# Attention scores in the two halves of the array's rows: three passes of 64 rows in place of two passes of 128

## The chip, the cores and the metric

The kernel runs on one core of a Trainium2 chip. The metric is the device time of one execution in microseconds (us). Before the change the median of three runs is 1358.63 us, the lowest 1357.41 and the highest 1358.8.

## What is computed

Two transformer blocks over 512 tokens of width 1024. The first has a stick-breaking attention with 16 heads of 64, a cross attention over 256 memory rows and a convolutional feed-forward; the second has three branches (a recurrent one with 8 heads of 64, a short convolution, a pooling) that are gated, merged and projected. The change touches the stick-breaking attention alone:

```
def stick_breaking_core(q, k, v):              # 16 heads of 64
    for start in range(0, seq, 128):
        end = start + 128
        z = einsum('bhtd,bhsd->bhts', q[start:end], k[:end]) * 64 ** -0.5
        earlier = arange(end)[None, :] < arange(start, end)[:, None]
        log_keep = where(earlier, log_sigmoid(-z), 0.0)
        csum = cumsum(log_keep, axis=-1)
        log_w = log_sigmoid(z) + (csum[..., -1:] - csum)
        w = where(earlier, exp(log_w), 0.0)
        outs.append(einsum('bhts,bhsd->bhtd', w, v[:end]))
```

## The kernel before

Every large product is done in three passes: an operand x is kept as two tiles of the type fp32r, its rounded value (hi) and the rest (lo), and hi·hi, hi·lo and lo·hi are added up in PSUM. `split_from` (L231) makes such a pair from PSUM: a copy on ACT for hi, a subtraction on DVE for lo. `mm3` (L217) issues the passes of a GEMM; its matmuls stand under L214. Weights arrive from memory in units of 512 KB and are split by `w_conv` (ACT L144, DVE L145), also fp32r.

**The order of the work.** The program writes its order out itself. A GEMM counts the array time that it has issued, and after each 1650 ns of it (eight matmuls of 512 columns, or 16 of 256) calls `tick` (L177). A tick advances the generators that run beside the GEMMs: each `yield n` lets n ticks pass. The numbers stand in the table `WAIT`. `drain` (L192) runs the generators to their end without GEMMs between.

**The attention.** The loop over eight pairs of heads, hp, computes q and k of a pair with two chunks of GEMM (`gemm_q`, `gemm_k`; `chunk` L245) and, over two pairs, v in four more (`gemm_v`). Then it drains the attention of the pair before and starts `attention(hp)` (L480) beside the GEMMs of the next pair. The last pair isn't drained at the start: its steps stand beside the chunks that compute the memory's keys (`ps_chunk<-memT`).

In `attention` a score is done in **two** passes of 128 rows. A head has only 64 rows, so the other 64 carry a second product: `gemm_q` puts a head's q hi into its own rows and its q lo into the other half; `gemm_k` puts k hi into both halves, and k lo into the own half beside rows that were zeroed once (`k_lo`, L435 to L437). The first pass gives hi·hi + lo·hi, the second hi·lo. For this q costs two copies on ACT of 64x512 and two subtractions on DVE, k four copies and two subtractions.

The steps of one pair, called here by these names; i is the block of 128 tokens whose scores are computed, and its product has (i+1)·128 columns:

- S1: block 1 of both heads, one bank of PSUM each
- S2 and S3 of head 0, then S2 and S3 of head 1: S2 is blocks 0 and 2 in one bank, S3 is block 3 in one bank, each at a place (a tick) of its own
- T: the transposes of the weights w, 20 of 128x128 in five groups of four, at three places; after each group a split of 128x512 on ACT and DVE
- V: the values, eight matmuls for each head, `values(0)` and `values(1)` at two places

After each S come, for each bank, a sigmoid on ACT (`keep`, L496), a scan on DVE (`r`, L498) and a subtraction on POOL (`w`, L500). Banks of PSUM: three with the tag g for GEMMs, two a, two b, one c. The scores use a, the transposes b and a, the values c and a.

Later in the kernel, in `rwkv_pair` (L1111), there are products of plain FP32 tiles that take 64 rows each, two heads by turns in the upper and the lower half of the rows, into two banks (`ps_ac`).

Of the kernel before, what the change touches and what calls it, by code (L numbers as in the profile page):

```python
# [68 lines left out]
def model_kernel(ctx: ExitStack, tc: tile.TileContext, a: dict, out: bass.AP, dbg: dict):  # L69
# [361 lines left out]

    def qk_tile(name):
        return att("qk", 7, name, dt=F32R)

    k_lo = [at.tile([P, S], F32R, name=f"kl{e}") for e in range(2)]  # L435
    for e in range(2):
        A.mul(k_lo[e][hrow(1 - e)], masks[hrow(1 - e), 0], 0.0)  # L437

    def gemm_q(ps=None):

        if ps is None:
            ps = chunk(xT)
        q = [qk_tile("q") for _ in range(2)]
        for e in range(2):
            A.copy(q[e][hrow(e)], ps[hrow(e)])
        for e in range(2):
            own = hrow(e)
            V.tensor_tensor(q[e][hrow(1 - e)], ps[own], f32(q[e][own]), ALU.subtract)
        return q

    def gemm_k(ps=None):

        if ps is None:
            ps = chunk(xT)
        k = [Split(qk_tile("kh"), lo) for lo in k_lo]
        for o in range(2):
            for e in range(2):
                A.copy(k[e].hi[hrow((e + o) % 2)], ps[hrow(e)])
        for e in range(2):
            own = hrow(e)  # L460
            V.tensor_tensor(k[e].lo[own], ps[own], f32(k[e].hi[own]), ALU.subtract)
        return k

# [16 lines left out]
    def attention(hp, q, k, vs):  # L480
        w, wT = {}, {}

        def scores(e, *parts):

            for z, part in enumerate((k[e].hi, k[e].lo)):
                for ps, i, o in parts:
                    n = (i + 1) * P
                    T.matmul(ps[:, o:o + n], q[e][:, tok(i)], part[:, 0:n],  # L488
                             start=z == 0 and o == 0, stop=z == 1 and i == parts[-1][1])

# [22 lines left out]

        pss = [bank("a", "ps_s") for _ in range(2)]
        for e in range(2):
            scores(e, (pss[e], 1, 0))
        t = weights_of(pss, 2)
        w[0, 1], w[1, 1] = (t, 0), (t, 256)
        yield wait["at0"]
        for e in range(2):  # L520
# [10 lines left out]
        def values(e):  # L531
            ps = bank("ca"[e], "ps_o")
            steps = []
            for j in range(4):
                s, n = wT[e, j]
                wid = (4 - j) * P
                lhs = vs[j][:, hp % 2, 2 * e:2 * e + 2, :].rearrange("p a d -> p (a d)")
                steps += [(z, j, lhs, part[:, n * P:n * P + wid]) for z, part in enumerate((s.hi, s.lo))]
            steps.insert(3, steps.pop(7))
            steps.insert(6, steps.pop(7))  # L540
            for z, j, lhs, part in steps:
                T.matmul(ps[:, j * P:S], lhs, part, start=(j == 0 and z == 0), stop=j == 2 and z == 1)  # L542
            own, oth = hrow(e), hrow(1 - e)
            A.copy(tmp[own], ps[oth])
            V.tensor_tensor(y[own], ps[own], tmp[own], ALU.add)
# [12 lines left out]
        values(1)  # L558
        split_to(y, yT.hi[:, hp], yT.lo[:, hp])
# [7 lines left out]
    for hp in range(NPAIR):  # L567
# [1010 lines left out]
```

## Time and profile before

| | before |
|---|---|
| median of three runs | 1358.63 us |
| the profiled execution | 1359.82 us |
| its span, first to last instruction | 1358.1 us |
| PE busy | 1328.8 us, 98% |
| weight loads (PEld) busy | 1112.2 us, 82% |
| DVE busy | 827.8 us, 61% |
| ACT busy | 527.9 us, 39% |
| POOL busy | 257.4 us, 19% |
| granted TensorE clock, mean | 0.993 |

The profile's times are in microseconds from the first instruction. PE are the matmuls and PEld the weight loads that run beside them. Matmuls overlap, so that a matmul's own length (0.39 us for 512 columns) is more than its share of the time: two that follow each other start 0.23 us apart. What a step costs is therefore read from one start to another.

### The profile page before, as it was taken

Reading aid. Unit: us, or ns where it says so; the run is one execution under the profiler, and the core shown is the slowest. Engines: PE = TensorE matmul, PEld = TensorE weight load, DVE = VectorE, ACT = ScalarE, POOL = GpSimd, SP = SyncE. Lnnn points to the kernel's source line nnn. Section 1 sums busy time; section 2 is a strip of 40 time slices with the busy share of each in tenths; the row PEclk is TensorE's granted clock in tenths of the full one; section 3 lists DMA queues with packets and bytes.
Section 4 is the critical chain, followed back from the end, with each engine's and each line's share of the span. In section 5 each row is a group of like instructions: output and inputs, shape, how many; then the busy total and the mean of one; then the engine's idle time right before and its main releaser. Section 6 shows DMA issues by size and latency. Waiting matters only on the chain.

```text
span 1358.1 us, 19442 instructions
## 1 busy us (share of the span) xinstructions
PE 1328.8 (98%) x7804; PEld 1112.2 (82%) x7804; DVE 827.8 (61%) x1425; ACT 527.9 (39%) x780; POOL 257.4 (19%) x244
## 2 busy tenths in 40 slices
PE   8999999999999999999999999999999989999997
PEld 7988888788879888888888888888878768887876
DVE  5787887765577555522556866666335567743575
ACT  6565665144423444321344235532323434222330
POOL 1333432000000434400132211200001342000230
PEclk9999999999999999999999999999999899999999
DMA  5121343242223333233234113234221223422331
GB/s 190 63 90 55 105 148 125 85 148 94 82 74 125 111 94 106 93 103 98 94 124 161 50 57 106 77 107 109 78 79 62 70 76 92 114 89 78 117 132 63
DMA packets 54666, 133.25 MB, mean 98 GB/s; under 512 B 19632, under 2 KB 21552, under 8 KB 54576
## 3 DMA queue, kind: packets, MB, share of 16 engines
q1 hardware_dynamic: 54576, 132.01, 30.7%
q8 instruction: 61, 1.00, 0.3%
q14 instruction: 29, 0.24, 0.1%
HBM read 126.48 MB, written 5.24 MB: 97 GB/s over the span
## 4 chain that ended last, share of the span: by engine, by line
PE 83%; DVE 10%; ACT 3%; DMA 2%; issue 1%; POOL 0%; DVEq 0%; SPq 0%; ACTq 0%; POOLq 0%
PE ps_chunk L214 48%; PE ps_rows L214 9%; PE ps_d L214 6%; PE ps_br L214 3%; PE ps_v L214 3%; PE ps_lead L214 3%; DVE wl L145 2%; PE ps_s L488 1%; PE ps_o L542 1%; ACT wh L144 1%; DVE lnt L650 1%; PE ps_t L510 1%; PE ps_z L214 1%; PE ps_o L214 1%; DMA wr<-in_w_xq_dram 1%
## 5 line engine op out<-in xcount | busy, mean ns | idle before, releaser
L145 DVE TENSOR_TENSOR wl<-wr,wh 128x1024 fp32r<-128x1024 f32 x196 | 251.8, 1286 | 144.5 <-ACT wh L144 143.9
L144 ACT CAST wh<-wr 128x1024 fp32r<-128x1024 f32 x196 | 204.9, 1046 | 116.9 <-PE ps_d L214 51.2
L214 PE MATMUL ps_chunk<-h3Th,wh 128*128 128x512 f32 x480 | 126.0, 398 | 0.0
L214 PE MATMUL ps_chunk<-h3Tl,wh 128*128 128x512 f32 x480 | 125.8, 397 | 0.0
L214 PE MATMUL ps_chunk<-h3Th,wl 128*128 128x512 f32 x480 | 124.3, 395 | 0.0
L872 DVE SCALAR_TENSOR_TENSOR c<-ps_chunk,colp,c 128x511 f32<-128x511 f32 x80 | 59.9, 749 | 92.2 <-ACT c L870 90.7
L878 POOL TENSOR_TENSOR c<-c 128x512 f32<-128x512 f32 x21 | 42.5, 2023 | 357.9 <-ACT c L877 209.3
L214 PEld LDWEIGHTS ps_chunk<-h3Th,wh 128*128 128x128 f32 x480 | 90.0, 190 | 21.1 <-issue 2.3
L214 PEld LDWEIGHTS ps_chunk<-h3Tl,wh 128*128 128x128 f32 x480 | 90.0, 190 | 19.8 <-issue 0.8
L214 PEld LDWEIGHTS ps_chunk<-h3Th,wl 128*128 128x128 f32 x480 | 89.6, 189 | 18.9
L214 PE MATMUL ps_chunk<-h2Th,wh 128*128 128x512 f32 x320 | 79.0, 389 | 0.0
L214 PE MATMUL ps_chunk<-h2Tl,wh 128*128 128x512 f32 x320 | 79.0, 389 | 0.0
L214 PE MATMUL ps_chunk<-h2Th,wl 128*128 128x512 f32 x320 | 79.0, 389 | 0.0
L500 POOL TENSOR_TENSOR w<-r 128x511 f32<-128x511 f32 x40 | 58.7, 1468 | 85.4 <-DVE r L498 76.7
L870 ACT ACTIVATE c<-ps_chunk,colp 128x512 f32<-128x512 f32 x40 | 31.1, 779 | 109.7 <-PE ps_chunk L214 109.7
L214 PEld LDWEIGHTS ps_chunk<-h2Th,wl 128*128 128x128 f32 x320 | 60.1, 188 | 12.5
L214 PEld LDWEIGHTS ps_chunk<-h2Tl,wh 128*128 128x128 f32 x320 | 60.1, 188 | 12.5
L214 PEld LDWEIGHTS ps_chunk<-h2Th,wh 128*128 128x128 f32 x320 | 60.0, 188 | 12.4
L498 DVE TENSOR_TENSOR_SCAN r<-keep,masks 128x512 f32<-128x512 f32 x40 | 59.8, 1509 | 12.5 <-ACT keep L496 8.0
L214 PE MATMUL ps_chunk<-xTh,wh 128*128 128x512 f32 x128 | 35.6, 402 | 5.3 <-ACT xTh L376 5.3
L214 PE MATMUL ps_d<-wh,gvb 128*128 128x512 f32 x128 | 39.7, 389 | 0.0
L496 ACT ACTIVATE keep<-ps_s 128x512 f32<-128x512 f32 (+1 forms) x48 | 24.5, 526 | 37.8 <-PE ps_s L488 37.7
(396 smaller groups left out, 2623.6 us busy)
## 6 DMA issues: line engine op xcount, KB each, us to landing
wr<-in_w_in_dram SPq DMA_DIRECT2D x65, 512.0 KB, 3.6
wr<-in_w_ff_dram SPq DMA_DIRECT2D x44, 512.0 KB, 3.6
wr<-in_w_dn_dram SPq DMA_DIRECT2D x22, 512.0 KB, 3.5
wr<-in_w_qk_dram SPq DMA_DIRECT2D x14, 512.0 KB, 3.5
wr<-in_w_br_dram SPq DMA_DIRECT2D x12, 512.0 KB, 3.5
wr<-in_w_v_dram SPq DMA_DIRECT2D x8, 512.0 KB, 3.7
wr<-in_w_xk_dram SPq DMA_DIRECT2D x8, 512.0 KB, 4.0
wr<-in_w_o_dram SPq DMA_DIRECT2D x8, 512.0 KB, 3.5
```

Of the source, the lines that this page charges most:

```text
L144: A.copy(w.hi, raw)
L145: lo_of.tensor_tensor(w.lo, raw, f32(w.hi), ALU.subtract)
L214: T.matmul(ps, l, r, start=start, stop=stop)
L488: T.matmul(ps[:, o:o + n], q[e][:, tok(i)], part[:, 0:n], start=z == 0 and o == 0, stop=z == 1 and i == parts[-1][1])
L496: A.activation(keep[:, j * n:(j + 1) * n], ps[:, 0:n], AF.Sigmoid, scale=-0.125)
L498: V.tensor_tensor_scan(r[:, ::-1], keep[:, ::-1], masks[:, m, ::-1], 1.0, ALU.mult, ALU.max)
L500: G.tensor_tensor(t[:, 0:S - 1], r[:, 1:S], r[:, 0:S - 1], ALU.subtract)
L510: T.transpose(ps[:, n], src[:, o + j * P:o + (j + 1) * P], ident)
L542: T.matmul(ps[:, j * P:S], lhs, part, start=(j == 0 and z == 0), stop=j == 2 and z == 1)
L870: A.activation(c, ps, AF.Identity, scale=cw(2), bias=col("ffb", j))
L872: V.scalar_tensor_tensor(c[:, 2 - r:S], ps[:, 0:S - 2 + r], cw(r), c[:, 2 - r:S], ALU.mult, ALU.add)
L878: (V if end else G).tensor_tensor(cv, cg, cv, ALU.mult)
```

## The change

The scores are done in three passes of 64 rows, hi·hi, hi·lo and lo·hi. Both heads of a pair are issued by turns, the even head with rows 0 to 63 and the odd one with rows 64 to 127, each into its own bank with the tag a. `gemm_q` and `gemm_k` become one `gemm_qk`, which splits the whole 128x512 with one copy and one subtraction; the zeroed tiles go. S2 and S3 are now one place each for both heads, T has two places instead of three, V has one place instead of two, and the second head's values go to a bank with the tag g. Of the table, `at2` goes from 1 to 3 and `at4` from 1 to 2. Nothing else of the program is changed.

```
-    "ss": 2, "us": 3, "ye": 4, "yo": 3, "yt": 1, "at0": 1, "at1": 1, "at2": 1, "at3": 1, "at4": 1,
+    "ss": 2, "us": 3, "ye": 4, "yo": 3, "yt": 1, "at0": 1, "at1": 1, "at2": 3, "at3": 1, "at4": 2,
...
-    k_lo = [at.tile([P, S], F32R, name=f"kl{e}") for e in range(2)]
-    for e in range(2):
-        A.mul(k_lo[e][hrow(1 - e)], masks[hrow(1 - e), 0], 0.0)
...
-        q = [qk_tile("q") for _ in range(2)]
-        for e in range(2):
-            A.copy(q[e][hrow(e)], ps[hrow(e)])
-        for e in range(2):
-            own = hrow(e)
-            V.tensor_tensor(q[e][hrow(1 - e)], ps[own], f32(q[e][own]), ALU.subtract)
-        return q
...
-        k = [Split(qk_tile("kh"), lo) for lo in k_lo]
-        for o in range(2):
-            for e in range(2):
-                A.copy(k[e].hi[hrow((e + o) % 2)], ps[hrow(e)])
-        for e in range(2):
-            own = hrow(e)
-            V.tensor_tensor(k[e].lo[own], ps[own], f32(k[e].hi[own]), ALU.subtract)
-        return k
+        s = Split(att("qk", 8, "qkh", dt=F32R), att("qk", 8, "qkl", dt=F32R))
+        split_from(ps, s.hi, s.lo)
+        return s
...
-        def scores(e, *parts):
-
-            for z, part in enumerate((k[e].hi, k[e].lo)):
-                for ps, i, o in parts:
-                    n = (i + 1) * P
-                    T.matmul(ps[:, o:o + n], q[e][:, tok(i)], part[:, 0:n],
-                             start=z == 0 and o == 0, stop=z == 1 and i == parts[-1][1])
+        def scores(*parts):
+
+
+            pss = [bank("a", "ps_s") for _ in range(2)]
+            for z, (l, r) in enumerate(((q.hi, k.hi), (q.hi, k.lo), (q.lo, k.hi))):
+                for i, o in parts:
+                    n = (i + 1) * P
+                    for e in range(2):
+                        T.matmul(pss[e][:, o:o + n], l[hrow(e), tok(i)], r[hrow(e), 0:n],
+                                 start=z == 0 and o == 0, stop=z == 2 and i == parts[-1][0])
+            return pss
...
-        for e in range(2):
-            ps = bank("a", "ps_s")
-            scores(e, (ps, 0, 0), (ps, 2, P))
+        for e, ps in enumerate(scores((0, 0), (2, P))):
             t = weights_of([ps], 0)
             w[e, 0], w[e, 2] = (t, 0), (t, P)
-            yield wait["at0"]
-            ps = bank("a", "ps_s")
-            scores(e, (ps, 3, 0))
+        yield wait["at1"]
+        for e, ps in enumerate(scores((3, 0))):
             w[e, 3] = (weights_of([ps], 1), 0)
-            yield wait["at1"] if e == 0 else wait["at2"]
...
+        yield wait["at2"]
         group("b", [(0, i, 0) for i in range(4)])
         group("b", [(0, 1, 1), (0, 2, 1), (0, 3, 1), (0, 3, 3)])
         yield wait["at3"]
         group("a", [(0, 2, 2), (0, 3, 2), (1, 2, 2), (1, 3, 2)])
-        yield wait["at3"]
+        group("a", [(1, 1, 1), (1, 2, 1), (1, 3, 1), (1, 3, 3)])
         group("b", [(1, i, 0) for i in range(4)])
-        group("a", [(1, 1, 1), (1, 2, 1), (1, 3, 1), (1, 3, 3)])
+        yield wait["at4"]
         y, tmp = att("y", 1, "y"), att("keep", 2, "yt")
-        yield wait["at4"]
-        values(0)
-        yield wait["at5"]
-        values(1)
+        order = [(z, j) for j in range(4) for z in range(2)]
+        order.insert(3, order.pop(7))
+        order.insert(6, order.pop(7))
+        for e in range(2):
+            ps = bank("cg"[e], "ps_o")
```

**On the tensor engine, at the first S1** (a piece of the difference; q and kh, kl are the tiles of before, qkh and qkl hi and lo of q and k now):

```order
 L214 MATMUL ps_chunk<-xTl,wh 128x512 x8
-L488 MATMUL ps_s<-kh,q 128x256
-L488 MATMUL ps_s<-kl_158,q 128x256
-L488 MATMUL ps_s<-kh,q 128x256
-L488 MATMUL ps_s<-kl_159,q 128x256
+L467 MATMUL ps_s<-qkh 128x256 x2
+L467 MATMUL ps_s<-qkl,qkh 128x256 x2
+L467 MATMUL ps_s<-qkh,qkl 128x256 x2
 L214 MATMUL ps_chunk<-xTh,wl 128x512 x8
```

Four matmuls have become three pairs; GEMM matmuls stand before and behind them as they did.

**On the vector engine, one pair of heads,** from its first scan to its last split of T. The kernel before:

```order
L498 SCALAR_TENSOR_TENSOR r<-keep,masks 128x512 x2
L477 TENSOR_TENSOR v<-ps_v,v 128x2x128
L498 SCALAR_TENSOR_TENSOR r<-keep,masks 128x512
L145 TENSOR_TENSOR wl<-wr,wh 128x1024
L498 SCALAR_TENSOR_TENSOR r<-keep,masks 128x512
L145 TENSOR_TENSOR wl<-wr,wh 128x1024
L498 SCALAR_TENSOR_TENSOR r<-keep,masks 128x512
L448 TENSOR_TENSOR q<-ps_chunk,q 64x512 x2
L233 TENSOR_TENSOR wtl<-ps_t,wth 128x512 x2
L145 TENSOR_TENSOR wl<-wr,wh 128x1024
L233 TENSOR_TENSOR wtl<-ps_t,wth 128x512 x3
```

And the same pair now:

```order
L478 SCALAR_TENSOR_TENSOR r<-keep,masks 128x512 x3
L453 TENSOR_TENSOR v<-ps_v,v 128x2x128
L478 SCALAR_TENSOR_TENSOR r<-keep,masks 128x512 x2
L145 TENSOR_TENSOR wl<-wr,wh 128x1024 x2
L233 TENSOR_TENSOR qkl<-ps_chunk,qkh 128x512
L233 TENSOR_TENSOR wtl<-ps_t,wth 128x512 x2
L145 TENSOR_TENSOR wl<-wr,wh 128x1024
L233 TENSOR_TENSOR wtl<-ps_t,wth 128x512 x3
```

The five scans (rows named r) stand in two batches with one subtraction between them; the subtractions for weights (wl) stood between the scans and now follow them. Head 0's S3 scan was the third of the pair and is now the fourth.

**On the tensor engine, where the last two pairs meet:** first the kernel before, then the change.

```order
L214 MATMUL ps_chunk<-memT,wl 128x256 x5
L510 MATMUL ps_t<-ident,w 128x128 x8
L488 MATMUL ps_s<-kh,q 128x256
L488 MATMUL ps_s<-kl_158,q 128x256
L488 MATMUL ps_s<-kh,q 128x256
L488 MATMUL ps_s<-kl_159,q 128x256
```

```order
L490 MATMUL ps_t<-ident,w 128x128 x12
L214 MATMUL ps_chunk<-memT,wh 128x256 x10
L214 MATMUL ps_chunk<-memT,wl 128x256 x5
L467 MATMUL ps_s<-qkh 128x256 x2
L467 MATMUL ps_s<-qkl,qkh 128x256 x2
L467 MATMUL ps_s<-qkh,qkl 128x256 x2
```

The last pair's S1 followed the transposes of the pair before at once; 15 matmuls of a GEMM now stand between them.

## Rows read from the trace of the kernel before

**Rows 1.** The page: its first part (busy time), and the chain that ended last by engine

```profile
PE 1328.8 (98%) x7804; PEld 1112.2 (82%) x7804; DVE 827.8 (61%) x1425; ACT 527.9 (39%) x780; POOL 257.4 (19%) x244
...
PE 83%; DVE 10%; ACT 3%; DMA 2%; issue 1%; POOL 0%; DVEq 0%; SPq 0%; ACTq 0%; POOLq 0%
```

**Rows 2.** Timeline of PE, second pair: start, length, instruction; S1, S2, S3 and the next GEMM

```profile
58.69 0.28 PE L488 MATMUL ps_s<-kh,q 128*128 128x256 f32 x1
...
59.15 1.11 PE L214 MATMUL ps_v<-wl,xTh 128*128 128x256 f32 x8
...
61.05 0.45 PE L488 MATMUL ps_s<-kh,q 128*128 128x128 f32 x2
...
61.62 2.01 PE L214 MATMUL ps_chunk<-xTh,wh 128*128 128x512 f32 x8
63.47 0.40 PE L488 MATMUL ps_s<-kh,q 128*128 128x512 f32 x1
...
63.94 1.97 PE L214 MATMUL ps_chunk<-xTl,wh 128*128 128x512 f32 x8
```

**Rows 3.** Lines by form, up to 230 us: copies and splits on ACT and DVE

```profile
L232 ACT CAST wth<-ps_t 128x512 fp32r<-128x512 f32 x40 | 21.9, 590 | 18.2 <-PE ps_t L510 18.1
...
L458 ACT CAST kh<-ps_chunk 64x512 fp32r<-64x512 f32 x32 | 18.5, 580 | 0.3
...
L461 DVE TENSOR_TENSOR kl<-ps_chunk,kh 64x512 fp32r<-64x512 f32 x16 | 11.0, 689 | 7.6 <-ACT kh L458 7.4
```

**Rows 4.** The tile ps_ac (64 rows, two heads by turns): length min/median/max in ns

```profile
L1111 PE MATMUL ps_ac<-misc,kb x128: 272/272/373, 854.6 to 1122.2; 64*128 64x128 f32 x128
```

**Rows 5.** Timeline of PE around one visit to ps_ac, from three windows

```profile
1114.64 0.62 PE L214 MATMUL ps_chunk<-h3Tl,wh 128*128 128x512 f32 x2
...
1115.11 0.85 PE L214 MATMUL ps_chunk<-h3Tl,wh 128*128 128x512 f32 x3
1115.88 1.16 PE L1111 MATMUL ps_ac<-misc,kb 64*128 64x128 f32 x16
1116.97 0.73 PE L214 MATMUL ps_chunk<-h3Tl,wh 128*128 128x512 f32 x2
```

**Rows 6.** Timeline of PE around plain FP32 products that take all 128 rows

```profile
803.23 1.05 PE L664 MATMUL ps_hT<-diag,hp 128*128 128x128 f32 x8
804.03 0.48 PE L214 MATMUL ps_lead<-h3Th,lead_w 128*128 128x256 f32 x2
```

**Rows 7.** Timeline of PE, last pair's S1, where PE stood still

```profile
195.84 1.04 PE L510 MATMUL ps_t<-ident,w 128*128 128x128 f32 x8
197.42 0.39 PE L488 MATMUL ps_s<-kh,q 128*128 128x256 f32 x1 [0.54 <-DVE wtl L233]
...
198.73 0.28 PE L214 MATMUL ps_chunk<-memT,wl 128*128 128x256 f32 x1
```

**Rows 8.** Timeline of PE, last pair: S3 of head 1, and a transpose of the third group

```profile
210.31 0.39 PE L488 MATMUL ps_s<-kl,q 128*128 128x512 f32 x1
...
216.91 0.33 PE L510 MATMUL ps_t<-ident,w 128*128 128x128 f32 x1 [1.43 <-POOL w L502]
```

**Rows 9.** Timelines of ACT and of PE behind the attention: the output projection and its weights

```profile
230.90 1.05 ACT L144 CAST wxh<-wr 128x1024 fp32r<-128x1024 f32 x1 [0.46 <-POOL yTl L237]
...
244.53 0.47 PE L214 MATMUL ps_rows<-wxh,yTh 128*128 128x512 f32 x1 [0.68 <-issue]
```

**Rows 10.** Timelines of DVE, POOL and PE, second pair: from S2 to the transposes

```profile
62.58 1.22 DVE L498 TENSOR_TENSOR_SCAN r<-keep,masks 128x512 f32<-128x512 f32 x1 [1.42 <-POOL w L502]
...
65.99 1.19 DVE L145 TENSOR_TENSOR wl<-wr,wh 128x1024 fp32r<-128x1024 f32 x1
67.23 1.94 DVE L498 TENSOR_TENSOR_SCAN r<-keep,masks 128x512 f32<-128x512 f32 x1
...
66.22 1.87 POOL L500 TENSOR_TENSOR w<-r 128x511 f32<-128x511 f32 x1 [1.06 <-DVE r L498]
...
70.48 1.04 PE L510 MATMUL ps_t<-ident,w 128*128 128x128 f32 x8
```

More of the change, by code (lines that the diff above doesn't have):

```diff
@@ L430, in model_kernel, with gemm_qk @@
                         compare_op=ALU.is_gt, fill=1.0, base=0, channel_multiplier=1)
-    def qk_tile(name):
-        return att("qk", 7, name, dt=F32R)
-    k_lo = [at.tile([P, S], F32R, name=f"kl{e}") for e in range(2)]
-    for e in range(2):
-        A.mul(k_lo[e][hrow(1 - e)], masks[hrow(1 - e), 0], 0.0)
-    def gemm_q(ps=None):
+    def gemm_qk(ps=None):
         if ps is None:
             ps = chunk(xT)
-        q = [qk_tile("q") for _ in range(2)]
-        for e in range(2):
-            A.copy(q[e][hrow(e)], ps[hrow(e)])
-        for e in range(2):
-            own = hrow(e)
-            V.tensor_tensor(q[e][hrow(1 - e)], ps[own], f32(q[e][own]), ALU.subtract)
-        return q
-    def gemm_k(ps=None):
-        if ps is None:
-            ps = chunk(xT)
-        k = [Split(qk_tile("kh"), lo) for lo in k_lo]
-        for o in range(2):
-            for e in range(2):
-                A.copy(k[e].hi[hrow((e + o) % 2)], ps[hrow(e)])
-        for e in range(2):
-            own = hrow(e)
-            V.tensor_tensor(k[e].lo[own], ps[own], f32(k[e].hi[own]), ALU.subtract)
-        return k
+        s = Split(att("qk", 8, "qkh", dt=F32R), att("qk", 8, "qkl", dt=F32R))
+        split_from(ps, s.hi, s.lo)
+        return s
     vws = []
@@ L512, in group @@
             split_from(ps.rearrange("p a b -> p (a b)"), s.hi, s.lo)
-        pss = [bank("a", "ps_s") for _ in range(2)]
-        for e in range(2):
-            scores(e, (pss[e], 1, 0))
-        t = weights_of(pss, 2)
+        t = weights_of(scores((1, 0)), 2)
         w[0, 1], w[1, 1] = (t, 0), (t, 256)
         yield wait["at0"]
-        for e in range(2):
-            ps = bank("a", "ps_s")
-            scores(e, (ps, 0, 0), (ps, 2, P))
+        for e, ps in enumerate(scores((0, 0), (2, P))):
             t = weights_of([ps], 0)
             w[e, 0], w[e, 2] = (t, 0), (t, P)
-            yield wait["at0"]
-            ps = bank("a", "ps_s")
-            scores(e, (ps, 3, 0))
+        yield wait["at1"]
+        for e, ps in enumerate(scores((3, 0))):
             w[e, 3] = (weights_of([ps], 1), 0)
-            yield wait["at1"] if e == 0 else wait["at2"]
[L531 to L545, printed above, removed]
+        yield wait["at2"]
         group("b", [(0, i, 0) for i in range(4)])
@@ L550, in attention @@
         group("a", [(0, 2, 2), (0, 3, 2), (1, 2, 2), (1, 3, 2)])
-        yield wait["at3"]
+        group("a", [(1, 1, 1), (1, 2, 1), (1, 3, 1), (1, 3, 3)])
         group("b", [(1, i, 0) for i in range(4)])
-        group("a", [(1, 1, 1), (1, 2, 1), (1, 3, 1), (1, 3, 3)])
+        yield wait["at4"]
         y, tmp = att("y", 1, "y"), att("keep", 2, "yt")
-        yield wait["at4"]
-        values(0)
-        yield wait["at5"]
-        values(1)
+        order = [(z, j) for j in range(4) for z in range(2)]
[3 more added lines that the diff above has]
+            ps = bank("cg"[e], "ps_o")
+            for z, j in order:
+                s, n = wT[e, j]
+                T.matmul(ps[:, j * P:S], vs[j][:, hp % 2, 2 * e:2 * e + 2, :].rearrange("p a d -> p (a d)"),
+                         (s.hi, s.lo)[z][:, n * P:n * P + (4 - j) * P], start=(z, j) == (0, 0), stop=(z, j) == order[-1])
+            own, oth = hrow(e), hrow(1 - e)
+            A.copy(tmp[own], ps[oth])
+            V.tensor_tensor(y[own], ps[own], tmp[own], ALU.add)
         split_to(y, yT.hi[:, hp], yT.lo[:, hp])
@@ L574, in model_kernel @@
         if hp:
-            q = gemm_q()
-            k = gemm_k()
+            q = gemm_qk()
+            k = gemm_qk()
         else:
@@ L583, in model_kernel @@
             w_done(2)
-            q, k = gemm_q(pss[0]), gemm_k(pss[1])
+            q, k = gemm_qk(pss[0]), gemm_qk(pss[1])
         if hp == 0:
```

## The prediction

> **What bounds the kernel now.** I read the page first: the tensor engine (PE) is busy 98% of the span, and 83% of the chain that ended last stands on it; DVE has 10%, ACT 3% [rows 1]. So in the attention, too, what counts is what stands in PE's own stream and how often PE stands still; work taken from ACT and DVE counts only where PE waits for it. Then I read the timeline of PE over one pair of heads. The scores stand between GEMM matmuls without a gap, and a step costs the distance from its first start to the start of the next GEMM [rows 2]: S1 0.46 us (58.69 to 59.15), S2 0.57 us (61.05 to 61.62), S3 0.47 us (63.47 to 63.94). S2 and S3 come twice, so a pair costs 0.46 + 2 × 0.57 + 2 × 0.47 = 2.54 us, and eight pairs 20.3 us. Third, the change's form of a product, 64 rows, two heads by turns, two banks, already stands elsewhere in this kernel: the tile ps_ac [rows 4, 5]. Last I looked for the places where PE stands still near the attention [rows 7 to 9].
>
> **Term 1, the scores themselves: −5.1 us.** Before, one pass over S1's two heads is two matmuls, and S1's 0.46 us holds four. If the halves run side by side, a pair of 64-row matmuls costs what one of 128 rows does. Does the trace show them side by side? A visit to ps_ac has 16 matmuls from 1115.88; the last ends 1.16 us later and is itself 0.27 us long, so it starts at 1116.77 [rows 4, 5]. The first is 0.10 us longer than the others (373 against 272 ns). That leaves (0.89 − 0.10) / 7 = 0.113 us for each pair, what a single plain product of 128 rows and the same 128 columns takes: eight last 1.05 us and the last of them 0.27, so (1.05 − 0.27) / 7 = 0.11 us each [rows 6]. So yes. Now a pair of heads costs three passes of one slot: S1 0.115, S2 0.285, S3 0.235, together 0.635 us, times three 1.91 us. Saved: 2.54 − 1.91 = 0.63 us, in eight pairs 5.1 us.
>
> **Term 2, going into the halves and out again: +9.4 us.** The same visit shows it [rows 5]. Normally a GEMM matmul of 512 columns starts 0.23 us after the one before (two take 0.62 us, of which the last is 0.39). Into ps_ac: the third matmul from 1115.11 should be followed at 1115.80; ps_ac starts at 1115.88, 0.08 to 0.09 us late, and its first pair takes 0.10 us more. Out of it: the last pair starts at 1116.77 and should be followed at 1116.88; the GEMM starts at 1116.97, 0.09 us late, and its first two matmuls take 0.73 instead of 0.62 us, 0.11 us more. Together 0.19 + 0.20 = 0.39 us for one visit. Plain FP32 products over all 128 rows show nothing of this: after ps_hT two GEMM matmuls are done at 804.51, and eight products of 0.11 and two of 0.12 us with the last one's 0.28 reach the same time [rows 6]. So the price goes with the 64 rows. Every S of the change stands between GEMM matmuls or values of 128 rows, three visits for a pair, 24 in all: 24 × 0.39 = 9.4 us. The bounds: nothing (if the price belonged to something else of ps_ac) and 0.39 us.
>
> [...]
>
> **Term 3, ACT and DVE: 0 us directly.** Six copies of 64x512 for a pair, 0.58 us each, become two of 128x512, 0.59 us each; four subtractions of 0.69 us become two [rows 3]. In eight pairs ACT loses 48 × 0.58 − 16 × 0.59 = 18 us and DVE 16 × 0.69 = 11 us. It is hidden: in the second pair PE goes on from score to GEMM without waiting [rows 2]. If the cover were gone, PE would wait for q and k at S1, but 16 GEMM matmuls stand there ahead of it.
>
> **Term 4, places where PE stands still: −2.7 us.** The last pair's S1 follows the transposes, and both its banks must first be emptied. Eight transposes of 0.11 us from 195.84 end at 196.72 and S1 takes 0.46, so the GEMM could go on at 197.18; it does at 198.73. That is 1.55 us lost [rows 7]. Now 15 GEMM matmuls, 1.8 us, stand between. I leave 0.3 us of the wait. In the last pair's third group a transpose waits 1.43 us for POOL; its weights are ready 6.4 us after the S3 of head 1 ended (210.31 + 0.23 to 216.91) [rows 8]. Now the first transposes stand 45 matmuls of 256 columns (0.12 us each, 5.4 us) behind S3, and the fourth of them needs head 0's S3 at 5.7 us: about 0.7 us of wait. The third: the output projection waits 0.68 us at 244.53 for weights whose first conversion could start only when the attention's last tile was done, at 230.90 [rows 9]. V now ends 27 matmuls (3.2 us) earlier against the projection, so I drop this wait. Together 1.25 + 0.73 + 0.68 = 2.7 us.
>
> **Term 5, new waits: +0.8 us.** On DVE the scan of head 0's S3 is now the fourth of its pair and not the third. Counting from S2's end [rows 10]: the first scan starts 0.96 us later (61.62 to 62.58) and takes 1.22; two more beside POOL take 1.94 each; one subtraction 0.69 [rows 3] stands between; POOL takes 1.87, and 0.1 for zeros. That is 8.7 us. The transposes need it after 0.20 (out) + 1.85 (eight matmuls) + 0.19 (in) + 0.70 (S3) + 0.20 + 5.55 (three ticks) + 0.33 (three transposes) = 9.0 us. The slack is 0.3 us; before, these weights were ready at 68.1 and wanted at 70.48. With all three scans at 1.94 it is 0.4 us short. So 0 to 0.4 us in each pair; I take 0.1 us, as one of the three usually has no POOL work beside it. S3 needs both banks of S2 empty: two sigmoids of 0.6 us against the 1.85 us of the tick, no wait. The second head's values go to a bank of the GEMMs, whose last use is a whole chunk back; no wait either.
>
> **The sum.** −5.1 + 9.4 − 2.7 + 0.8 = +2.4 us. The profiled execution took 1359.82 us, so 1362.2 us on its scale; it lies 1.2 us above the median of the runs, 1358.63, and on that scale the forecast is 1361.0 us. About 0.2% (2.7 us) is what a measurement of this kernel can tell from no change, so the forecast is "no change, leaning to slower". Its own range runs from all three waits of term 4 gone and none new (−5.1 + 9.4 − 3.7 = +0.6, 1359.2 us) to none gone and 0.4 us new in each pair (−5.1 + 9.4 + 3.2 = +7.5, 1366.1 us).
>
> **Rivals.**
>
> *A. The visits cost nothing.* Then the sum is −5.1 − 2.7 + 0.8 = −7.0, 1351.6 us, clearly faster. For it: no row shows 64 rows of fp32r, and the weights that load behind ps_ac belong to another type. Against it: all visits to ps_ac have the same longest first matmul, and plain FP32 with 128 rows costs nothing. Chance 0.14.
>
> *B. The transposes wait in every pair (slower).* DVE is the place: if a weight subtraction of 1.19 us [rows 10] comes ahead of head 0's S3 scan, or POOL slows all scans, the slack of 0.3 us turns into a wait of up to 0.9 us in each pair: 8 × 0.9 = 7.2 instead of 0.8, 1367.4 us. It decides as soon as w is ready later than 9.0 us after S2's end. For it: the five scans are now in two batches. Against it: the order of DVE keeps the weight subtractions behind the second batch. Chance 0.13.
>
> *C. At full width the halves don't run side by side.* ps_ac has 128 columns of plain FP32; S3 has 512 of fp32r. If two such matmuls took turns, each slot would double: 8 × 1.91 = 15.3 us more, 1376.3 us. Chance 0.05.
>
> *D. The loads don't hide.* In the stream of ps_ac a pair costs 0.113 us although each half loads new weights between, so there they hide. If each slot but a visit's first paid the 0.10 us of an open load, 9 × 0.10 × 8 = 7.2 us would be added: 1368.2 us. Chance 0.04. [...]
>
> That the change doesn't do what it says I leave out: PE's order shows the pairs.
>
> **How the numbers follow.** The forecast has 0.64, A 0.14, B 0.13, C 0.05, D 0.04. The forecast's sum lies close to the bound of 2.7 us, so I split its 0.64 into 0.26 slower, 0.35 within and 0.03 faster (a visit at half its price). Faster: 0.14 + 0.03 = 0.17. Within: 0.35. Slower: 0.26 + 0.13 + 0.05 + 0.04 = 0.48. The range reaches from a price of a visit of about a fifth (1353.5) to B's 1367.5; it leaves out A's full gain, C and D, some 0.2.
>
> **What would show it.** In the profile after: ps_s with 192 matmuls, the first pair of each visit 0.10 us longer than it would be; S1 0.35, S2 0.86, S3 0.70 us, and around each visit 0.39 us more up to the second GEMM matmul; no wait at the last pair's S1 beyond 0.3 us; ACT some 17 and DVE some 11 us less busy. I am wrong if the distances around a visit are those of a GEMM (A), if PE waits for POOL at most transposes (B), or if a slot of S3 is near 0.47 us (C).

## The result and the profile after

The changed kernel takes **1366.6 us** (median of 4 runs, 1365.69 to 1369.2), the kernel before 1358.02 us in the same session (4 runs): a ratio of **1.0067**, 95% interval 1.0054 to 1.008. It is slower by 8.6 us (0.67%), more than the 2.7 us that such a measurement can tell from no change. The forecast was 1361.0 us, "no change, leaning to slower", with a range of 1353.5 to 1367.5; slower had the largest chance, 0.48. The profiled execution took 1369.2 us (span 1367.5).

The page of the kernel after, busy time and the chain that ended last by engine, answers to [rows 1]:

```profile
PE 1334.4 (98%) x7868; PEld 1106.8 (81%) x7868; DVE 821.0 (60%) x1409; ACT 507.1 (37%) x746; POOL 262.2 (19%) x244
...
PE 80%; DVE 11%; DMA 4%; ACT 3%; issue 2%; POOL 1%; DVEq 0%; SPq 0%; ACTq 0%; POOLq 0%
```

ACT is 20.8 us less busy and DVE 6.8, yet the chain stands on DVE and DMA more than before and on PE less. That is the first sign that new waits, and not only PE's own work, made the time.

**The scores.** Timeline of PE of the kernel after, second pair (start, length, instruction); it answers to [rows 2]:

```profile
58.30 1.00 PE L214 MATMUL ps_v<-wh,xTh 128*128 128x256 f32 x7
59.23 0.39 PE L467 MATMUL ps_s<-qkh 64*128 64x256 f32 x2
...
59.78 1.22 PE L214 MATMUL ps_v<-wl,xTh 128*128 128x256 f32 x8
...
61.89 0.55 PE L467 MATMUL ps_s<-qkh 64*128 64x128 f32 x4
...
62.95 2.11 PE L214 MATMUL ps_chunk<-xTh,wh 128*128 128x512 f32 x8
64.99 0.50 PE L467 MATMUL ps_s<-qkh 64*128 64x512 f32 x2
...
65.88 2.14 PE L214 MATMUL ps_chunk<-xTl,wh 128*128 128x512 f32 x8
```

S1 takes 0.55 us (59.23 to 59.78), S2 1.06, S3 0.89. By the forecast's terms: three slots each, 0.35, 0.86 and 0.70 us, and 0.10 + 0.09 us of a visit inside each distance give 0.54, 1.05 and 0.89. What lies outside is there too: the seventh ps_v starts at 58.30 + 1.00 − 0.28 = 59.02, S1 could follow at 59.14 and starts 0.09 us late; behind it eight ps_v take 1.22 us, where the eight behind the old S1 took 1.11 [rows 2]. All 24 visits of the trace look like these, but for the last pair's S3 (0.96 us). So terms 1 and 2 came out to a few hundredths of a us: 9.4 − 5.1 = 4.3 us in eight pairs.

**The last pair and the projection.** Timelines of PE of the kernel after, three windows; they answer to [rows 7 to 9]:

```profile
203.70 0.76 PE L214 MATMUL ps_chunk<-memT,wl 128*128 128x256 f32 x5
204.39 0.39 PE L467 MATMUL ps_s<-qkh 64*128 64x256 f32 x2
...
218.96 0.49 PE L490 MATMUL ps_t<-ident,w 128*128 128x128 f32 x3
221.01 0.77 PE L490 MATMUL ps_t<-ident,w 128*128 128x128 f32 x5 [1.55 <-POOL w L482]
...
223.40 1.03 PE L490 MATMUL ps_t<-ident,w 128*128 128x128 f32 x8
224.67 0.66 PE L490 MATMUL ps_t<-ident,w 128*128 128x128 f32 x4 [0.24 <-DVE wtl L233]
...
252.00 0.47 PE L214 MATMUL ps_rows<-wxh,yTh 128*128 128x512 f32 x1 [0.95 <-issue]
```

The wait at S1 is gone to the last hundredth (five matmuls of 0.12 us from 203.70 and the 0.09 of a visit end at 204.39). The wait of the transposes for POOL is not: the fourth could start at 219.29 and starts at 221.01, 1.72 us late, and a later group is 0.40 us late, 2.1 us in all; before they lost 1.60 us, of which 1.43 stood as idle. And the projection still waits for its weights, 0.95 us where it was 0.68.

**What is new.** Timeline of PE of the kernel after, second pair, transposes and values:

```profile
74.22 1.03 PE L490 MATMUL ps_t<-ident,w 128*128 128x128 f32 x8
75.48 0.66 PE L490 MATMUL ps_t<-ident,w 128*128 128x128 f32 x4 [0.23 <-DVE wtl L233]
...
79.08 0.40 PE L519 MATMUL ps_o<-wth,v 128*128 128x512 f32 x1
80.03 0.50 PE L519 MATMUL ps_o<-wtl,v 128*128 128x512 f32 x1 [0.55 <-DVE wtl L233]
```

The last group of transposes is 0.39 us late (eight from 74.22 at (1.03 − 0.27) / 7 = 0.109 us each end at 75.09), the second head's values 0.72 us (79.08 + 0.23 = 79.31). Both wait for DVE's wtl, the rests of the transposed weights. The same stands in the fourth pair (125.94; 129.89 and 131.09) and in the sixth (177.01; 181.46): together 1.2 us at the transposes and 2.6 at the values. With the first matmul behind each wait, which mostly takes 0.06 to 0.11 us longer than usual (the one of 512 columns 0.50 us instead of 0.39), it is **4.2 us**. No wait for w is there, where the forecast had looked.

Where does it come from? The same stretch on DVE, POOL, SP (DMA issues) and ACT, kernel after:

```profile
69.11 1.23 DVE L478 TENSOR_TENSOR_SCAN r<-keep,masks 128x512 f32<-128x512 f32 x1 [0.87 <-POOL w L480]
70.25 3.98 DVE L145 TENSOR_TENSOR wl<-wr,wh 128x1024 fp32r<-128x1024 f32 x2
...
78.10 1.88 DVE L233 TENSOR_TENSOR wtl<-ps_t,wth 128x512 fp32r<-128x512 f32 x3
...
69.23 1.94 POOL L480 TENSOR_TENSOR w<-r 128x511 f32<-128x511 f32 x1
71.17 1.98 POOL L480 TENSOR_TENSOR w<-r 128x511 f32<-128x511 f32 x1
...
72.27 2.31 SPq L123 DMA_DIRECT2D wr<-in_w_v_dram  x2
...
75.87 1.05 ACT L144 CAST wh<-wr 128x1024 fp32r<-128x1024 f32 x1 [2.67 <-DMA wr<-in_w_v_dram]
76.83 1.55 ACT L232 CAST wth<-ps_t 128x512 fp32r<-128x512 f32 x3
```

and of the kernel before, SP, and the second weight subtraction on DVE with POOL's w beside it (the first is in [rows 10]):

```profile
67.22 3.42 SPq L123 DMA_DIRECT2D wr<-in_w_v_dram  x2
...
69.09 1.19 DVE L145 TENSOR_TENSOR wl<-wr,wh 128x1024 fp32r<-128x1024 f32 x1
...
69.31 1.87 POOL L500 TENSOR_TENSOR w<-r 128x511 f32<-128x511 f32 x1 [1.19 <-DVE r L498]
```

Read it from the top. Both S3 scans now stand in a row on DVE, so the two weight subtractions wl come behind them, at 70.25 and not at 65.99 and 69.09, and behind POOL's w, beside which each takes 2.0 us instead of 1.19. A raw weight tile is free only after its wl, there are two of them, and so SP issues the load of w_v at 72.27 instead of 67.22. ACT stands 2.67 us for it, and in ACT's order this cast comes ahead of the copies wth of the last three groups of transposes; those start at 76.83, DVE's wtl at 78.10, and PE waits for the last of them until 80.03. The experiments test this chain.

### The profile page after: what moved, and what is told of

Same layout as the page of the kernel before. It is cut to its first block, busy times and chain, and to the rows that moved or that the text cites. A ratio compares the mean times of both kernels' runs of the same rounds, so it can differ in the third digit from the quotient of the medians.

```text
span 1367.5 us, 19506 instructions
## 1 busy us (share of the span) xinstructions
PE 1334.4 (98%) x7868; PEld 1106.8 (81%) x7868; DVE 821.0 (60%) x1409; ACT 507.1 (37%) x746; POOL 262.2 (19%) x244
## 4 chain that ended last, share of the span: by engine, by line
PE 80%; DVE 11%; DMA 4%; ACT 3%; issue 2%; POOL 1%; DVEq 0%; SPq 0%; ACTq 0%; POOLq 0%
PE ps_chunk L214 45%; PE ps_rows L214 9%; PE ps_d L214 6%; PE ps_v L214 3%; PE ps_br L214 3%; PE ps_lead L214 3%; DVE wl L145 3%; ACT wh L144 1%; PE ps_o L519 1%; PE ps_s L467 1%; DVE lnt L615 1%; DMA wr<-in_w_xq_dram 1%; POOL w L480 1%; PE ps_z L214 1%; PE ps_o L214 1%
## 5 line engine op out<-in xcount | busy, mean ns | idle before, releaser
L145 DVE TENSOR_TENSOR wl<-wr,wh 128x1024 fp32r<-128x1024 f32 x196 | 267.0, 1365 | 150.7 <-ACT wh L144 149.2
L480 POOL TENSOR_TENSOR w<-r 128x511 f32<-128x511 f32 x40 | 70.2, 1756 | 72.4 <-DVE r L478 62.7
L478 DVE TENSOR_TENSOR_SCAN r<-keep,masks 128x512 f32<-128x512 f32 x40 | 49.2, 1247 | 28.9 <-ACT keep L476 20.4
L1262 POOL TENSOR_TENSOR misc<-misc,rs_y 128x256 f32<-128x256 f32 x8 | 6.5, 838 | 160.4 <-DVE rs_y L285 160.4
```

The costliest lines, as they stand in the source:

```text
L145: lo_of.tensor_tensor(w.lo, raw, f32(w.hi), ALU.subtract)
L478: V.tensor_tensor_scan(r[:, ::-1], keep[:, ::-1], masks[:, m, ::-1], 1.0, ALU.mult, ALU.max)
L480: G.tensor_tensor(t[:, 0:S - 1], r[:, 1:S], r[:, 0:S - 1], ALU.subtract)
L1262: G.tensor_tensor(yt[:, q, :, e], yt[:, q, :, e], ri[:, e, q].unsqueeze(2).to_broadcast([P, NT, CH]), ALU.mult)
```

## The experiments

All times are medians, all ratios against the kernel before in the same session. "Attention" is the distance from the start of the first ps_s matmul to that of the first ps_rows matmul on PE (after: 34.47 to 234.54), which the spread of later stages doesn't touch; it is read from one profiled execution of each kernel.

| kernel | us (runs) | ratio, 95% interval | attention, us |
|---|---|---|---|
| before | 1358.02 (4) | | 192.80 |
| after | 1366.6 (4) | 1.0067 (1.0054 to 1.008) | 200.07 |
| e1 the places, two passes | 1360.55 (10) | 1.0021 (1.0012 to 1.0031) | 196.32 |
| e2 T and V at old places | 1369.19 (4) | 1.0082 (1.0067 to 1.0097) | 200.83 |
| e3 two visits a pair | 1363.78 (4) | 1.0044 (1.0027 to 1.0061) | 196.32 |
| e4 no turns | 1369.84 (2) | 1.0086 (1.0065 to 1.0106) | 201.91 |
| e5 scans of S3 apart | 1362.29 (10) | 1.0031 (1.0021 to 1.004) | 196.10 |
| e11 third raw tile | 1364.18 (4) | 1.0051 (1.0036 to 1.0066) | 197.11 |
| e12 its control | 1366.56 (4) | 1.0066 (1.0049 to 1.0083) | 200.10 |
| e7 e3 and e5 | 1361.22 (10) | 1.0024 (1.0014 to 1.0033) | 194.28 |
| e8 one visit a pair | 1357.68 (10) | 0.9999 (0.999 to 1.0009) | 191.49 |
| e9 e8, later transposes | 1357.56 (11) | 0.9998 (0.9989 to 1.0007) | 189.60 |
| e10 before, last pair later | 1354.06 (7) | **0.9972** (0.9962 to 0.9983) | 189.62 |

### e1 and e2: is it the half rows or the places?

e1 has all places of the change, those of the scores too, and the two passes, q and k of the kernel before (a piece of its difference stands first). e2 is the changed kernel with T and V at the places of before and `at4` at 1 again; its scores keep the changed places (second piece).

```diff
-            for z, (l, r) in enumerate(((q.hi, k.hi), (q.hi, k.lo), (q.lo, k.hi))):
+            for e in range(2):
+                for z, part in enumerate((k[e].hi, k[e].lo)):
...
-                        T.matmul(pss[e][:, o:o + n], l[hrow(e), tok(i)], r[hrow(e), 0:n],
+                        T.matmul(pss[e][:, o:o + n], q[e][:, tok(i)], part[:, 0:n],
```

```diff
         group("a", [(1, 1, 1), (1, 2, 1), (1, 3, 1), (1, 3, 3)])
+        yield wait["at3"]
         group("b", [(1, i, 0) for i in range(4)])
...
         for e in range(2):
             ps = bank("cg"[e], "ps_o")
+            if e:
+                yield wait["at5"]
```

> The places of the change (one for both heads' S2, one for S3, two for T, one for V), but the scores as before: two passes of 128 rows with the old copies of q and k. Theory A: the change's 8.6 us are two things, the visits to the half rows less the saved slots (about 4.2 us) and new waits of PE at T and V because DVE and the weights' conversion fall behind (about 4.2 us). Then this kernel loses the first and keeps the second: about 1362.5 us, or up to 1364 us as DVE has 11 us more to do. Rival P, the visits are all of it: 1358 us. Rival Q, the places are all of it: 1366.6 us.

> The half rows of the change, but T again at three places and V at two (one tick between them as before). Theory A: the waits at T and V in the second, fourth and sixth pair (0.4 us at the transposes and 0.6 to 1.3 us at the values, 4.2 us in all) go, the visits stay: about 1362.5 us. Rival P (visits alone): 1366.6 us. Rival Q (places alone): 1358 us.

e1 lost 2.6 us against the 1357.97 of its session. A wait on PE and the two wl on DVE, e1 and then e2, second pair:

```profile
75.17 0.66 PE L513 MATMUL ps_t<-ident,w 128*128 128x128 f32 x4 [1.03 <-DVE wtl L233]
...
69.00 3.98 DVE L145 TENSOR_TENSOR wl<-wr,wh 128x1024 fp32r<-128x1024 f32 x2
```

```profile
79.88 0.50 PE L522 MATMUL ps_o<-wtl,v 128*128 128x512 f32 x1 [0.58 <-DVE wtl L233]
...
70.02 3.98 DVE L145 TENSOR_TENSOR wl<-wr,wh 128x1024 fp32r<-128x1024 f32 x2
```

In e1 three pairs lose 1.2 us each at the transposes, and none at the values. In e2 T and V are back at their places, the wait at the values stays, and the last pair's S1, again right behind transposes, waits again (1.24 us idle at 205.74). Both missed their expectation: e1 lies between theory A (1362.5) and rival P (1358), e2 above all three. And they don't part what they were meant to part. In both, the scores stand at the changed places, so both S3 scans stand in a row on DVE, the two wl behind them take 2.0 us each, and the load of w_v goes out late (71.02 us in e1, 72.05 in e2, 67.22 before). What they do show: the half rows aren't needed for waits on wtl, and putting T and V back doesn't remove them. The places of the scores are tested only by e5. The two parts don't add: +3.5 and +8.0 us of attention apart, +7.3 together.

### e3: what is a visit worth?

S2 follows S1 at once, in banks of its own; 16 visits instead of 24.

```diff
-        t = weights_of(scores((1, 0)), 2)
+        first = scores((1, 0))
+        second = scores((0, 0), (2, P), tag="b")
+        t = weights_of(first, 2)
...
-        for e, ps in enumerate(scores((0, 0), (2, P))):
+        for e, ps in enumerate(second):
```

> The change with S1 and S2 in one visit to the half rows (S2 into the two banks b): 16 visits instead of 24, the same matmuls. Theory A, a price of 0.39 us for each visit: 3.1 us less, 1363.5 us, within 1 us as the scans come in another rhythm; no extra start or long first matmul between S1 and S2. Rival, the price goes with each matmul of 64 rows and not with the visit: 1366.6 us.

It takes 1363.78 us, 2.8 us less than after, and 8 × 0.39 = 3.1 us was the price. The time alone doesn't settle it, as e3 also moves S2's weights forward: its transposes of the second, fourth and sixth pair don't wait, while the last pair's wait longer (2.86 us idle instead of 1.55), and the attention is 3.75 us shorter. The visit itself does. Timeline of PE, e3, second pair:

```profile
58.17 0.39 PE L467 MATMUL ps_s<-qkh 64*128 64x256 f32 x2
...
59.57 1.21 PE L214 MATMUL ps_v<-wl,xTh 128*128 128x256 f32 x8
```

S1 and S2 take 1.40 us together where they took 0.55 + 1.06, which is 0.21 us less, and the 0.09 and 0.1 us outside a visit are paid once less: 0.4 us for a visit.

### e4: do the turns make the halves run side by side?

Head 0's three passes first, then head 1's:

```diff
-            for z, (l, r) in enumerate(((q.hi, k.hi), (q.hi, k.lo), (q.lo, k.hi))):
-                for i, o in parts:
-                    n = (i + 1) * P
-                    for e in range(2):
+            for e in range(2):
+                for z, (l, r) in enumerate(((q.hi, k.hi), (q.hi, k.lo), (q.lo, k.hi))):
+                    for i, o in parts:
+                        n = (i + 1) * P
```

> The change with the heads one behind the other in each visit (three passes of the even head, then three of the odd one) in place of by turns. Theory A: two matmuls run side by side only when neighbours in the stream lie in different halves; here nearly every slot stands alone, 8 x 1.91 = 15.3 us more, about 1382 us, and S3's six matmuls start 0.23 us apart. Rival C, fp32r at full width doesn't run side by side even by turns: no difference, 1366.6 us.

It takes 1369.84 us, 3.2 more than after and not 15. Timeline of PE of e4, S1 and S3 of the second pair:

```profile
60.33 0.39 PE L467 MATMUL ps_s<-qkh 64*128 64x256 f32 x2
60.56 0.29 PE L467 MATMUL ps_s<-qkl,qkh 64*128 64x256 f32 x2
60.67 0.29 PE L467 MATMUL ps_s<-qkh,qkl 64*128 64x256 f32 x2
...
66.49 0.51 PE L467 MATMUL ps_s<-qkh 64*128 64x512 f32 x2
```

These rows look like those of the changed kernel: S1 takes 0.56 us and S3 0.90, where it has 0.55 and 0.89. In the program head 1's first matmul is the fourth, but here it starts with head 0's first (x2; 60.333 and 60.343), ahead of head 0's second and third (60.56 and 60.67). (The trace holds starts and not the order in which PE received the matmuls, so by what rule head 1's came first is not shown. That this order did change is seen in S2, and in the 0.01 us between the two first starts, 0.002 in the changed kernel.) So the turns are not what makes the overlap in S1 and S3. In S2, where head 1's first matmul is the seventh, it starts 0.4 us behind head 0's, and S2 takes 1.45 us instead of 1.06, in all eight pairs: 8 × 0.39 = 3.1 us, about what the run is slower by. Rival C, two full-width products that take turns, is out as well.

### e5, e11, e12: the chain behind the new waits

e5 breaks the chain at the top: head 1's sigmoid, scan and w of S3 come one tick later, so that a weight subtraction gets between the two scans (its matmuls stay where they are; T then needs two ticks instead of three).

```diff
         for e, ps in enumerate(scores((3, 0))):
             w[e, 3] = (weights_of([ps], 1), 0)
-        yield wait["at2"]
+            yield 1 if e == 0 else wait["at2"]
```

> The change, but head 1's part of S3 (sigmoid, scan, subtraction) is issued one tick after head 0's, and T follows at the same tick as in the change. On DVE a weight subtraction then stands between S3's two scans, as before the change. Theory B2: the new waits come from both heads' scans standing in a row: the weights' subtractions come late, the raw tiles free late, the loads of the next weights (72.3 us in the second pair, 67.2 before) and their copy on ACT come late, and the splits of the last transposes queue behind that copy. Then the load comes about 2 us earlier, the waits at T and V in the second, fourth and sixth pair shrink from 1.2 to 1.6 us each to under 0.5, the output projection starts at 231.5 instead of 234.5 us, and the whole takes about 1363 us. Rival, the values wait because both heads stand at one place: 1366.6 us, waits unchanged.

It came out at 1362.29 us, 4.3 less than after. DVE, SP and PE of e5, second pair:

```profile
66.62 1.23 DVE L478 TENSOR_TENSOR_SCAN r<-keep,masks 128x512 f32<-128x512 f32 x1 [0.55 <-POOL w L480]
67.76 2.00 DVE L145 TENSOR_TENSOR wl<-wr,wh 128x1024 fp32r<-128x1024 f32 x1
69.68 2.06 DVE L478 TENSOR_TENSOR_SCAN r<-keep,masks 128x512 f32<-128x512 f32 x1
...
69.78 3.42 SPq L123 DMA_DIRECT2D wr<-in_w_v_dram  x2
...
73.82 1.47 PE L490 MATMUL ps_t<-ident,w 128*128 128x128 f32 x12
```

The first wl stands between the scans, the load goes out at 69.78 instead of 72.27, twelve transposes run through, and none of the waits of pairs 2, 4 and 6 is left. But e5 moves several things on DVE at once. e11 breaks only the link of the raw tiles: a third one, from the second pair to the seventh. It takes one tile of q and k for room; e12 has only that (the second pair of lines).

```diff
-            if sum(j not in own_raw for j in raws) >= RAW * len(raw_of):
+            if sum(j not in own_raw for j in raws) >= (3 if len(raw_of) == 3 else RAW * len(raw_of)):
...
-        s = Split(att("qk", 8, "qkh", dt=F32R), att("qk", 8, "qkl", dt=F32R))
+        s = Split(att("qk", 7, "qkh", dt=F32R), att("qk", 7, "qkl", dt=F32R))
...
+        if hp == 1:
+            ring = raw_of[0]
+            raw_of[:] = [ring, ring, lambda: at.tile([P, 1024], F32, tag="wr3", bufs=1, name="wr3")]
+        if hp == NPAIR - 1:
+            raw_of[:] = [ring]
```

> The changed kernel with a third raw tile for the weights from the second pair to the seventh (one tile fewer for q and k makes room). Theory (late weight subtractions on DVE keep the two raw tiles, so the loads of w_v start late, ACT's cast of them stands late in front of the copies of the transposes): the loads are issued by the first visits of the pair, ACT finds them there, the waits of T and V in pairs 2, 4 and 6 (4.2 us in all) go or fall below 1.5 us; output projection begins at about 230.5 to 232 (234.54 there), time 1362.5 to 1364 us. Rival (the rows on DVE and ACT are late by themselves: the subtractions wtl stand behind the slow scans and weight subtractions, whatever the loads do): waits stay, projection at 234 to 235, time 1366 to 1367 us.

> The changed kernel with seven instead of eight tiles for q and k and nothing else: what the room for the third raw tile costs by itself. Expected to be level with the changed kernel, 1366 to 1367.5 us, projection at 234.5; were it dearer, the third raw tile is to be read against this run.

e12 is level with after, so e11's 1364.18 is to be set against 1366.56: 2.4 us, and 3.0 us of attention. DVE, ACT and PE of e11, second pair:

```profile
70.76 3.98 DVE L145 TENSOR_TENSOR wl<-wr,wh 128x1024 fp32r<-128x1024 f32 x2
...
73.60 1.06 ACT L144 CAST wh<-wr 128x1024 fp32r<-128x1024 f32 x1
...
75.99 0.66 PE L490 MATMUL ps_t<-ident,w 128*128 128x128 f32 x4 [0.23 <-DVE wtl L233]
...
79.85 0.39 PE L519 MATMUL ps_o<-wtl,v 128*128 128x512 f32 x1
```

DVE is as late and as slow as ever (3.98 us for two), but ACT casts the weights at 73.60 without a wait, and the values go through without one, in all three pairs. So the wait at the values is the raw tiles' (late wl, late load, late cast in front of wth): **shown**. The 0.23 at the transposes stays, in all three pairs: that smaller part, 1.2 us in all, is put down to the late and slow wl on DVE itself, which wtl stands behind. No run breaks that link alone. The rival mechanism was right for that part alone.

### e7 to e10: how far can it be brought?

e7 is e3 and e5 together. e8 has S1, S2 and S3 in one visit and in six banks, and hands them to ACT in pieces; the first lines of its difference:

```diff
-        t = weights_of(scores((1, 0)), 2)
+        first, second, third = scores((1, 0)), scores((0, 0), (2, P), tags="bb"), scores((3, 0), tags="gc")
+        t = weights_of(first, 2)
...
```

> One visit for S1 and S2 (16 visits) and head 1's part of S3 a tick later. If both effects are what they are taken for, they add: 1363.8 less 3 us, about 1360.5 us; the output projection starts at about 227.5 us. Rival, the two share a cause (both only move DVE's queue): 1363 us, as each alone.

> One visit for S1, S2 and S3 of both heads (8 visits; S2 in the banks b, S3 in g and c), their sigmoids and scans spread over four ticks in the order S1, S3 of head 0, S2 of head 0, S2 of head 1, S3 of head 1, T and V at the change's places, the last pair's start two ticks later. Price of a visit 0.39 us: 16 less are 6.2 us; with the waits at T and V gone (3 us) 1357.4 us, level with the kernel before, the output projection starts at about 225 us. Rival, the bank g that a score holds stops the GEMM: a wait of PE at the next chunk, and 1360 us or more.

Both came within 0.8 us of what was expected. With eight visits instead of 24 and no wait in pairs 2, 4 and 6 the half rows are level with the kernel before, not better: 2.54 − 1.91 = 0.63 us are saved in a pair, and less 0.39 us for the one visit 0.24 us are left, 1.9 us in eight pairs. Of these the attention shows 1.3 us and the time nothing that stands clear of the spread, and the last pair's transposes still wait 1.76 and 1.42 us. Timeline of PE, e8, last pair, and then the stretch behind it (its bounds and length, the busy time of PE, PEld, DVE, ACT and POOL, the granted clock, the share and GB/s of DMA):

```profile
213.48 0.49 PE L490 MATMUL ps_t<-ident,w 128*128 128x128 f32 x3
215.56 0.76 PE L490 MATMUL ps_t<-ident,w 128*128 128x128 f32 x5 [1.59 <-POOL w L482]
217.57 0.79 PE L490 MATMUL ps_t<-ident,w 128*128 128x128 f32 x4 [1.25 <-DVE wtl L233]
...
218.80 3.21 PE L214 MATMUL ps_chunk<-memT,wh 128*128 128x256 f32 x16
...
218.00:221.40 3.40, 3.40 (x19) 3.40 (x17) 3.40 (x7) 2.00 (x3) 0.00 (x0) 0.51 0.66 224
```

The last two rows show more: the granted clock is 0.51 there, where it is 1.00 over the attention of before and of after; PE had stood still for 1.59 and 1.25 us ahead of it. 27 GEMM matmuls of 256 columns from 218.01 on take 4.8 us instead of 27 × 0.12 = 3.2, so 1.5 us of e8's attention are clock. e7's has such a stretch too (0.51 from 213.3 to 216.8, behind a wait of 2.92 us); the attention of the other kernels has none.

So e9 issues these transposes one tick later (they then have GEMM work of the memory keys ahead of them that can cover the wait). e10 does the like in the kernel before, without half rows: the last pair's attention starts one tick later (`as7` 3 instead of 2), and head 1's S3 of it is followed by another tick. First e9 against e8, then e10 against before:

```diff
-        yield wait["at2"]
+        yield wait["at2"] + (hp == NPAIR - 1)
```

```diff
-            yield wait["at1"] if e == 0 else wait["at2"]
+            yield wait["at1"] if e == 0 else wait["at2"] + (hp == NPAIR - 1)
```

> One visit per pair with the last pair's transposes one tick of the memory projection later. Theory (what is left in the single-visit kernel is 1.76 + 1.42 us of waits of the last pair's transposes for the weights w from POOL): both shrink, output projection begins at about 222.5 to 224 (225.35 there), time about 1355.5 us (1354.5 to 1356.5). Rival (the wait only moves on, to the values or to the output projection that follows them): projection begins at 225.4 again, time 1357.5 us or more.

> The kernel before (two passes of 128 rows, its own places) with head 1's scores of the last pair one tick later, so that the transposes behind them find their weights. Tells whether a gain of the single-visit kernel with late transposes is of the half rows or of the last pair alone. If the waits of the last pair (1.25 before S1 stays, 1.43 + 0.73 before the transposes go) can be covered by the memory projection without half rows: about 1356 us, projection begins at 225.5 to 226.5 (227.33 before). If the wait only moves on: 1358 us, 227.3.

e9 missed its expectation. One row of PE's timeline, last pair:

```profile
219.45 0.66 PE L490 MATMUL ps_t<-ident,w 128*128 128x128 f32 x4 [1.72 <-DVE wtl L233]
```

The wait for POOL is gone, but this one is longer (1.88 us late), and a GEMM matmul ahead of it is 0.85 us late behind DVE's kT (215.17): 2.7 us, where e8's transposes lost 3.2. e9's attention is 1.9 us shorter than e8's, but 1.5 of that is the clock, which e9's execution has in full there and at 0.51 from 785.4 to 788.9 us. Its time is the same: its trace loses 1.8 us elsewhere (0.5 ahead of the attention, 0.4 at the projection, whose wait grew from 0.90 to 1.30 us, 0.9 behind it). So the runs don't show what later transposes are worth with half rows.

e10 beats both kernels, by 3.7 us against before. Its S1 and its transposes on PE's timeline, last pair:

```profile
199.05 0.28 PE L488 MATMUL ps_s<-kh,q 128*128 128x256 f32 x1
...
216.29 0.60 PE L510 MATMUL ps_t<-ident,w 128*128 128x128 f32 x4
...
218.52 1.07 PE L510 MATMUL ps_t<-ident,w 128*128 128x128 f32 x8
```

No row of the last pair has a wait: the 1.55 us at S1 and the 1.60 us at the transposes [rows 7, 8] are gone, 3.15 of the 3.18 us by which its attention is shorter. What the change got right (the S1 wait) needs one number in the table of waits and no half rows. (e10's attention is as long as e9's. The 3.5 us between their times lie outside it and stay open.)

## Why the prediction was right, and where it was not

- **Term 1 (slots, −5.1) and term 2 (visits, +9.4): right.** The sizes were read from a tile of another stage and another type, ps_ac. That they hold for fp32r and 512 columns was an estimate; the runs show it: S1, S2 and S3 within 0.01 us of the forecast, a visit 0.39 us, and e3's visit of S1 and S2 together saves 0.4 us. Rivals A, C and D fall with it. The way into the half rows and the way out both cost time, now for fp32r too (0.09 us late on either side of S1).
- **Term 3 (ACT and DVE directly, 0): right as far as it went.** ACT lost 20.8 us of work (18 forecast), DVE 6.8 (11 forecast): the scans got 10.6 us cheaper (59.8 to 49.2 us on the two pages), as more of them now start ahead of POOL's w (37 of 40 take under 1.3 us, 23 before), and wl 15.2 us dearer (251.8 to 267.0), as more of them start behind it. Of these 15.2 us the attention has two thirds: its 35 subtractions of L145 take 43.3 us before and 53.7 after. The rest lies in later stages. That exchange is what term 5 missed.
- **Term 4 (waits gone, −2.7): half right.** The S1 wait went wholly, 1.55 instead of 1.25. The step on the third group failed: I took w to be ready 6.4 us behind S3 as before and wanted at 5.7. It is wanted at 5.8 (219.29), but ready only 7.5 us behind S3's end at 213.48: on DVE head 0's S3 scan comes behind the two S2 scans, a wl of 1.99 us (215.04) and kT, at 217.40, and on POOL its w starts at 219.15 and takes 1.80 us. So the wait grew by 0.5 us instead of shrinking by 0.73. And the projection's wait did not go (0.95 us). I had read the first of the four casts of its weights [rows 9]. The last one counts: the profile names no releaser for PE, but in all twelve traces that wait here PE starts 0.70 to 0.83 us after the end of the fourth subtraction wxl, and the cast ahead of it waits for its load in both kernels (ACT idle 3.03 us before 241.40, and 2.30 us before 248.99 in the kernel after). The end of V isn't on that path.
- **Term 5 (new waits, +0.8): the step that failed most, 4.2 us.** I priced whether w comes in time for the first transposes, and it does. I did not follow what else stands behind the scans on DVE: rival B's sentence "the order of DVE keeps the weight subtractions behind the second batch" was taken as reassurance, and it is the cause. The rival had the engine right, but the wrong instruction as victim. In place of +0.8 us for w the runs show 4.2 us for wtl, 2.9 of them at the values by way of the raw tiles (e11: 3.0 us of attention).

The sum in the attention, by what was measured: +4.3 (terms 1 and 2), −1.55 (S1), +0.5 (last pair's transposes), +4.2 (new waits) = +7.45 against 7.27 us between the two traces. The two traces differ by 9.4 us in all, the medians by 8.6. The rest lies behind the attention: 0.3 us at the projection's wait, 0.9 us before the tile ps_z (66.71 us from the projection's first wxh matmul to it, 65.80 before; 65.9 in e1 and e10, 66.05 to 66.44 in the other kernels with half rows) and 1.0 us behind it. These differ from trace to trace, and their cause stays open.

The forecast's sum was +2.4 us and the measured difference is 8.6. That the time fell inside the range is partly luck: the range's upper end was B's price, and the waits came by another road than B's.

## What to carry to other kernels

Before joining two pieces of work that stand apart, look at what runs between them on the side engines: here a weight subtraction freed a buffer for a load, and the load's cast stood ahead of copies that PE needed, four links from the scan that was moved. A visit to half rows cost 0.39 us here, and a whole pair's scores saved 0.63 us: it pays only if much is done in one visit, so count visits and not matmuls alone. And when a change removes a wait as a by-product, try to remove the wait by itself first: e10 gained with two numbers what the change did not.

## What the hardware showed that was not expected

- **Matmuls of the other half started ahead of the program's order** (e4 above: the fourth starts at 60.343 us, the second at 60.56).
- **Of wl on DVE and w on POOL, the one that started later took longer.** In the kernel before wl starts ahead of w and takes 1.19 us, and w takes 1.87 instead of the 1.04 of one alone; in the kernel after w starts first and wl takes 2.0. In e5 both stand in one pair: the wl that starts behind a w takes 2.00 us (67.76), the one that starts ahead of a w 1.19 (71.66). In the kernel after the ends stand at a fixed distance: w ends at 71.17 and the first wl at 72.27 (SP's issue), 1.1 us later; the next w ends at 73.15 and the two wl at 74.23, again 1.1 us later, about what a wl that starts first takes in all (1.19). What makes the later one longer the rows don't show. So the same wl costs 0.8 us more where it now starts behind a w.
